# Matrix product of differenced running sums: when the first rows are started, and in which DMA queue their last stores wait

## The chip, the cores and the metric

One core of one Trainium2 chip runs the kernel. The metric is the device time of one execution in microseconds (us). A run here means one execution; a median is over several of them.

## The reference, cut to what matters

```python
# x: (8, 2048, 2048) float32, w: (2048, 2048) float32
cs = np.cumsum(x, axis=1)
diff = cs - shifted(cs)            # shifted by one row, a zero row first
return np.matmul(diff, w)
```

A running sum minus the running sum one row earlier is the row itself. So the kernel computes out = x times w: 16384 rows, 128 row tiles of 128 rows.

## The kernel before

It works in three stages.

1. *First rows.* Row tiles 0 to 3 (512 rows) are multiplied in bf16, while w streams in from memory in 32 blocks: 16 for the left half of the columns, 16 for the right half. TensorE itself transposes this part of x.
2. *First group.* Once all of w is there, it is scaled by its largest magnitude and narrowed to f16. Row tiles 4 to 7 form the first group. From here on the products are by Strassen and Winograd, two levels, so besides matmuls there are sums of quarters of x and w on VectorE (S1 to S4, T1 to T4), evictions of results on ScalarE (`keep`), additions of results on VectorE (`add`), and stores (`put`).
3. *The rest.* Tiles 8 to 127 in groups of four; the group of tiles 8 to 11 is called second.

Before a row tile can be multiplied it passes a chain: load (SyncE queue), magnitude (ScalarE), scale from it (VectorE), narrowing to f16 (ScalarE), and a transposing DMA (SyncE queue), which the program calls a turn. In these traces SyncE's DMAs are in one queue (q1, 345.56 MB in the kernel before), GpSimd's in another (q0, 4.20 MB), and ScalarE's, where it issues any, in a third (q10, 0.52 MB); the text also calls such a queue a ring.

The end of the first rows, where the stores of the right half are put in a queue (cuts marked with `...`):

```python
def put(c, rows, columns):
    nc.gpsimd.dma_start(out2[rows, columns], c)
...
measure_4(PLAIN + 2, x6)                 # magnitude of tile 6, in four pieces
finish_row(1)
...                                      # load of tile 5 into x5
turned_6 = narrow_turn(PLAIN + 2, x6)    # turn of tile 6 (SyncE queue)
x7, _ = after("sp", lambda: bring(PLAIN + 3))   # load of tile 7 (SyncE queue)
finish_row(2)
...
finish_row(3)
with tc.issue_after(turned_6.ins):
    for c, rows, columns in done:        # eight pieces of 256 KB
        put(c, rows, columns)            # GpSimd queue
...
left_over(bank(2))                       # the ninth piece: computed, stored
...                                      # magnitude of tile 5
narrow_turn(PLAIN + 1, x5)               # turn of tile 5 (SyncE queue)
```

The call `issue_after` did not keep these stores behind the turn: in the profile before, GpSimd issues four of them at 68.11 and 71.95 us, and the turn of tile 6 is issued at 74.07.

The first group (`g` is tile 4, `h` is tile 6), with the lines that the argument needs:

```python
product(X, A11g, B11, True)          # tile 4
...
keep(C11g, X, ug)                    # lies where the stored pieces were
product(V, A12g, B21, True)
product(Y, A11h, B11, True)          # tile 6: needs its turn
add(C11g, V, ug)
...
total(S1, A21g, A22g, ADD)           # needs the turn of tile 5
product(Z, A12h, B21, True)
weigh(h + 1, d)                      # magnitude of tile 7: needs its load
...
product(V, S1, T1, True)             # called S1*T1 below
...
weigh(g + 4, a)                      # magnitude of tile 8
product(X, A21g, T3, False)
total(S1, A21h, A22h, ADD)
total(S2, S1, A11h, SUB)
add(C11h, Z, uh)
put(C11h, h, 0)
scale_of(g + 4)                      # scale of tile 8 (VectorE)
ready(g + 4)                         # narrow it
turn(g + 4)                          # turn it
add(C12g, V, ug)
put(C12g, g, 1)
fetch_x(g + 5)                       # load of tile 9
...
weigh(g + 5, c)                      # magnitude of tile 9
scale_of(g + 5)
keep(C22, Z, vh)                     # eviction that a later product waits for
```

## Time and profile before

| quantity | before |
|---|---|
| time, median of 3 (lowest to highest) | 1512.86 us (1511.98 to 1514.31) |
| span of the profiled execution | 1511.4 us |
| TensorE busy | 1493.6 us (99%) |
| VectorE, ScalarE, GpSimd busy | 73%, 57%, 1% |
| hardware queue of SyncE, share of 16 DMA engines | 79.9% |
| first matmul of tile 4 | 72.7 us |
| first matmul of S1*T1 | 95.20 us |
| matmul behind the wait in the second group | 145.12 us |

The last three rows are marks on TensorE's timeline. The kernel is bound by TensorE from end to end, so a change can only be read by how much earlier TensorE passes such a mark. The lines themselves are shown in the prediction. In them `fin` is a loaded row tile of x (tile 5 is loaded into `xP`), `xT` a turned one, `b` a bank of TensorE's results, `c` a result tile, and `o` a stored piece of the first rows (two of them go by `wb`, the name of w's cast blocks). Line numbers move with the change: the eviction is L492 before and L497 after, the addition L497 before and L502 after.

### The profile page before, as it was taken

Reading aid. Unit: us, or ns where it says so; the run is one execution under the profiler, and the core shown is the slowest. Engines: PE = TensorE matmul, PEld = TensorE weight load, DVE = VectorE, ACT = ScalarE, POOL = GpSimd, SP = SyncE. Lnnn points to the kernel's source line nnn. Section 1 sums busy time; section 2 is a strip of 40 time slices with the busy share of each in tenths; the row PEclk is TensorE's granted clock in tenths of the full one; section 3 lists DMA queues with packets and bytes.
Section 4 is the critical chain, followed back from the end, with each engine's and each line's share of the span. In section 5 each row is a group of like instructions: output and inputs, shape, how many; then the busy total and the mean of one; then the engine's idle time right before and its main releaser. Section 6 shows DMA issues by size and latency. Waiting matters only on the chain.

```text
span 1511.4 us, 19128 instructions
## 1 busy us (share of the span) xinstructions
PE 1493.6 (99%) x6906; PEld 674.7 (45%) x6912; DVE 1104.4 (73%) x2052; ACT 866.8 (57%) x1116; POOL 11.9 (1%) x21
## 2 busy tenths in 40 slices
PE   8999999999999999999999999999999999999998
PEld 3434444444444444444444444444444444444443
DVE  7887777676777676776677776767776767777767
ACT  5866555556555656555556555665555565556551
POOL 0200000000000000000000000000000000000000
PEclk9999999999999999999999999999999999999999
DMA  9987878878888888888789788778787888887772
GB/s 362 347 227 232 241 218 249 226 218 235 236 228 237 213 227 237 218 249 235 204 234 242 214 247 223 226 233 240 220 237 211 235 226 240 239 233 218 224 209 111
DMA packets 321903, 351.50 MB, mean 233 GB/s; under 512 B 266896, under 2 KB 266896, under 8 KB 305936
## 3 DMA queue, kind: packets, MB, share of 16 engines
q1 hardware_dynamic: 320240, 345.56, 79.9%
q0 software_dynamic: 1280, 4.20, 0.8%
q8 instruction: 54, 0.88, 0.2%
q10 hardware_dynamic: 288, 0.52, 0.1%
q14 instruction: 41, 0.34, 0.1%
HBM read 150.99 MB, written 134.22 MB: 189 GB/s over the span
## 4 chain that ended last, share of the span: by engine, by line
PE 89%; DVE 1%; issue 0%; DVEq 0%; ACT 0%
PE b L463 53%; PE b L474 36%; DVE c L497 1%; DVE W L506 0%; DVE W L510 0%; DVEq L929 0%; ACT b L548 0%; DVE xT L506 0%; DVE s L112 0%; DVE m L111 0%; DVE u L581 0%; DVE m L556 0%; DVEq L497 0%
## 5 line engine op out<-in xcount | busy, mean ns | idle before, releaser
L497 DVE SCALAR_TENSOR_TENSOR c<-b,u,c 128x512 f32<-128x512 f32 (+1 forms) x883 | 675.2, 800 | 237.4 <-ACT c L492 115.3
L492 ACT ACTIVATE c<-b,u 128x512 f32<-128x512 f32 x496 | 314.8, 679 | 272.7 <-PE b L463 174.8
L463 PE MATMUL b<-W,xT 128*128 128x512 f16 x2048 | 464.1, 380 | 4.3 <-DMA xT<-fin 3.3
L463 PE MATMUL b<-W,W 128*128 128x512 f16 x1764 | 411.7, 379 | 0.0
L105 ACT ACTIVATE c<-fin 128x2048 f16<-128x2048 f32 x92 | 175.6, 1909 | 246.9 <-DMA out_dram<-c 235.9
L463 PEld LDWEIGHTS <-xT 128*128 128x128 f16 x2048 | 200.7, 98 | 248.1 <-DMA xT<-fin 4.5
L463 PEld LDWEIGHTS <-W 128*128 128x128 f16 x2016 | 197.3, 98 | 238.0 <-issue 0.3
L116 ACT ACTIVATE fin<-fin,s 128x2048 f16<-128x2048 f32 x123 | 246.3, 2002 | 88.7 <-issue 49.8
L474 PEld LDWEIGHTS <-W 128*128 128x128 f16 x1560 | 152.2, 98 | 187.0 <-issue 2.0
L474 PE MATMUL b<-W,W 128*128 128x512 f16 x810 | 219.8, 379 | 0.7 <-DVE c L497 0.5
L474 PE MATMUL b<-W,xT 128*128 128x512 f16 x720 | 180.0, 379 | 0.1
L474 PE MATMUL b<-inner,W 128*128 128x512 f16 x660 | 176.2, 379 | 0.0
L474 PEld LDWEIGHTS <-xT 128*128 128x128 f16 x960 | 93.9, 98 | 113.3
L556 DVE TENSOR_REDUCE m<-m 128x1 f32<-128x4 f32 x29 | 4.6, 157 | 103.2 <-ACT b L548 103.2
L463 PE MATMUL b<-W 128*128 128x512 f16 x252 | 74.9, 379 | 0.0
L548 ACT ACTIVATE b<-fin 128x512 f32<-128x512 f32 x116 | 67.9, 585 | 10.1 <-DMA fin<-in_x_dram 9.8
L506 DVE TENSOR_TENSOR W<-W,xT 128x1024 f16<-128x1024 f16 x122 | 68.1, 558 | 3.2
L506 DVE TENSOR_TENSOR W<-xT,W 128x1024 f16<-128x1024 f16 x122 | 67.4, 552 | 0.0
L474 PE MATMUL b<-inner,xT 128*128 128x512 f16 x240 | 61.6, 379 | 0.0
L233 PE MATMUL b<-wb,xP 128*128 128x512 bf16 x234 | 56.0, 388 | 3.7 <-ACT wb L216 2.9
L506 DVE TENSOR_TENSOR W<-xT,xT 128x1024 f16<-128x1024 f16 (+1 forms) x92 | 54.8, 596 | 0.0
L111 DVE TENSOR_SCALAR m<-m 128x1 f32<-128x1 f32 x124 | 18.5, 149 | 37.4 <-ACT c L105 36.2
(55 smaller groups left out, 467.6 us busy)
## 6 DMA issues: line engine op xcount, KB each, us to landing
out_dram<-c SPq DMA_DIRECT2D x247, 512.0 KB, 3.1
fin<-in_x_dram SPq DMA_DIRECT2D x123, 1024.0 KB, 5.5
W<-in_w_dram SPq DMA_DIRECT2D x32, 512.0 KB, 9.3
W<-in_x_dram SPq DMA_DIRECT2D x16, 256.0 KB, 7.5
out_dram<-o POOLq DMA_DIRECT2D x14, 256.0 KB, 5.1
xT<-fin SPq DMA_TRANSPOSE x184, 5.1
xP<-in_x_dram SPq DMA_DIRECT2D x1, 1024.0 KB, 8.0
out_dram<-wb POOLq DMA_DIRECT2D x2, 256.0 KB, 6.9
```

What stands on the lines that cost most here:

```text
L105: return m, nc.scalar.activation(waste.bitcast(f16), xf, ABS, scale=1.0 / ROW, accum_out=m)
L111: nc.vector.tensor_scalar(m, m, TINY, None, MAX)
L116: return xh, nc.scalar.activation(xh, xf, COPY, scale=s)
L233: lambda: nc.tensor.matmul(ps[r][n], xP[:, r, ko, :], wb[h, ko][:, ds(n * NB, NB)], start=(ko == 0), stop=(ko == KO - 1),),
L463: nc.tensor.matmul(ps[n], a[k], b[k][:, n, :], start=(first and k == 0), stop=(k == KH - 1), skip_group_check=True,)
L474: nc.tensor.matmul(ps, a[k], b[k], start=(first and k == 0), stop=(k == 3), skip_group_check=True)
L492: after("act", lambda: nc.scalar.activation(c, p, COPY, scale=scale))
L497: "dve", lambda: nc.vector.scalar_tensor_tensor(c, p, scale, c, MUL, ADD)
L506: after("dve", lambda: nc.vector.tensor_tensor(dst.all, p.all, q.all, op))
L548: lambda: nc.scalar.activation(ps[i % 2], xf[:, at], ABS, scale=1.0 / ROW, accum_out=m4[:, i : i + 1],),
L556: after("dve", lambda: nc.vector.tensor_reduce(m, m4, AX.X, ADD))
```

## The change

The intent: let the first rows begin before all of their x is there; get the stores of the right half out of the way of the turn of tile 6; shorten the way to that turn; and let the magnitude of a tile of the third group go ahead of an eviction. There are four parts. (a) The start: x of rows in pairs around the first block of w.

```diff
-    WARM = 8
+    WARM = 7
...
-        loads = {0: 0, 2: 1, 5: 2, 9: 3}
+        loads = {2: 1, 5: 2, 9: 3}
         for ko in range(KO):
             if ko in loads:
                 load_x(loads[ko])
+            if ko < 2:
+                load_x(0, range(2 * ko, 2 * ko + 2))
             fetch(0, ko)
-        xb = cast_x(0)
-        v = [turn_x(xb, a, 6 + a) for a in range(2)]
-        turned(0, 0, v[0], "act")
-        turned(0, 1, v[1], "dve")
         for ko in range(KO - KQ):
+            if ko == 0:
+                for a in range(2):
+                    xb = cast_x(0, [a])
+                    turned(0, a, turn_x(xb, a, 6 + a), "dve")
+                    if a == 0:
+                        taken(0, ko)
+                    for r in (2 * a, 2 * a + 1):
+                        plain(0, r, ko)
+                continue
```

(b) The stores: from the GpSimd queue to the SyncE queue, behind the turn of tile 6 and ahead of the turn of tile 5. The load of tile 7 goes to the end.

```diff
-            put(c, ds((PLAIN - 1) * P, P), ds(NB, NB))
+            done.append((c, ds((PLAIN - 1) * P, P), ds(NB, NB)))
...
-        turned_6 = narrow_turn(PLAIN + 2, x6)
-        x7, _ = after("sp", lambda: bring(PLAIN + 3))
+        narrow_turn(PLAIN + 2, x6)
...
-        with tc.issue_after(turned_6.ins):
-            for c, rows, columns in done:
-                put(c, rows, columns)
...
         left_over(bank(2))
+        for c, rows, columns in done:
+            after("sp", lambda: put(c, rows, columns, nc.sync))
...
         narrow_turn(PLAIN + 1, x5)
+        x7, _ = after("sp", lambda: bring(PLAIN + 3))
```

(c) Magnitudes of tiles 4 and 6 in two pieces of 1024 instead of four of 512.

```diff
-            for i in range(4):
-                at = ds(i * NB, NB)
+            for i in range(2):
+                at = ds(i * NH, NH)
```

(d) The order of two steps in the second group.

```diff
         product(Y, A11h, B11, True)
+        if second:
+            weigh_in(g + 4, V)
         C11h = new_c(b)
         keep(C11h, Y, uh)
-        weigh_in(g + 4, V)
+        if not second:
+            weigh_in(g + 4, V)
```

More of the change, by code (lines that the diff above doesn't have):

```diff
@@ L172, with load_x @@
             )
-        def load_x(q):
-            for r in range(PLAIN):
+        def load_x(q, rows=range(PLAIN)):
+            for r in rows:
                 nc.sync.dma_start(
@@ L179, in load_x, with cast_x @@
                 )
-        def cast_x(q):
+        def cast_x(q, pairs=range(2)):
             xb = resting(q, 0).bitcast(bf16).rearrange("p (a c) -> p a c", a=2)
-            for a in range(2):
+            for a in pairs:
                 after(
@@ L240, in plain, with put @@
                 )
-        def put(c, rows, columns):
-            nc.gpsimd.dma_start(out2[rows, columns], c)
+        def put(c, rows, columns, queue=nc.gpsimd):
+            return queue.dma_start(out2[rows, columns], c)
         def plain_out(h, r):
@@ L335, in block, with measure_2 @@
                 )
-        waste = first.tile([P, NB], f16, name="waste")
+        waste = first.tile([P, NH], f16, name="waste")
         got = {}
         scales = {}
-        def measure_4(t, xf):
-            m = small.tile([P, 1], f32, name="m")
-            m4 = small.tile([P, 4], f32, name="m4")
-            for i in range(4):
-                at = ds(i * NB, NB)
+        def measure_2(t, xf):
+            m, m2 = (small.tile([P, n], f32, name=i) for n, i in ((1, "m"), (2, "m2")))
+            for i in range(2):
+                at = ds(i * NH, NH)
                 after(
@@ L349, in measure_4 @@
                     lambda: nc.scalar.activation(
-                        waste, xf[:, at], ABS, scale=1.0 / ROW, accum_out=m4[:, i : i + 1]
+                        waste, xf[:, at], ABS, scale=1.0 / ROW, accum_out=m2[:, i : i + 1]
                     ),
                 )
-            after("dve", lambda: nc.vector.tensor_reduce(m, m4, AX.X, ADD))
+            after("dve", lambda: nc.vector.tensor_reduce(m, m2, AX.X, ADD))
             scales[t], _ = after("dve", lambda: invert(m))
@@ L382, in left_over @@
             after("act", lambda: nc.scalar.activation(c, ps, COPY, scale=uw))
-            put(c, ds((PLAIN - 1) * P, P), ds(NB, NB))
+            done.append((c, ds((PLAIN - 1) * P, P), ds(NB, NB)))
         for k in range(4):
             block(B11, 0, 0, k, "dve")
-        measure_4(PLAIN, x4)
+        measure_2(PLAIN, x4)
         for k in range(4, KH):
@@ L393 @@
             block(B21, 1, 0, k, "dve")
-        measure_4(PLAIN + 2, x6)
+        measure_2(PLAIN + 2, x6)
         finish_row(1)
```

## The prediction

> **What bounds the kernel now.** I began with the page. TensorE is nearly full:
>
> ```profile
> PE 1493.6 (99%) x6906; PEld 674.7 (45%) x6912; DVE 1104.4 (73%) x2052; ACT 866.8 (57%) x1116; POOL 11.9 (1%) x21
> ```
>
> The span is 1511.4 us, so everything that could be gained without taking away matmuls is 17.8 us of idle, plus any time in which matmuls run slowly. By stage, TensorE is busy 1305.9 of the last 1312 us; all that this change touches lies before 200 us. The view of TensorE's waits names nearly all of the idle time:
>
> ```profile
> PE b L463 <- DMA xT<-fin: 3.3, 1, 3.3
> PE b L233 <- ACT wb L216: 2.9, 7, 0.8
> PE b L195 <- DVE W L186: 2.6, 1, 2.6
> PE b L258 <- DVE xP L158: 1.2, 1, 1.2
> PE b L463 <- ACT c L492: 0.8, 1, 0.8
> PE b L474 <- DVE c L497: 0.5, 1, 0.5
> ```
>
> One hole of 3.3 us stands out. The timeline around it (start, duration, engine, operation) shows why:
>
> ```profile
> 72.03 2.01 ACT L116 ACTIVATE fin<-fin,s 128x2048 f16<-128x2048 f32 x1
> 74.07 4.84 SPq L127 DMA_TRANSPOSE xT<-fin  x1
> 74.81 3.02 POOL L243 DMA_DIRECT2D out_dram<-o  x4 [1.62 <-ACT o L251]
> 79.00 1.46 SPq L99 DMA_DIRECT2D fin<-in_x_dram  x1
> 82.33 6.83 SPq L127 DMA_TRANSPOSE xT<-xP  x2
> 86.60 8.77 PE L463 MATMUL b<-W,xT 128*128 128x512 f16 x32 [3.35 <-DMA xT<-fin]
> 89.35 1.26 ACT L492 ACTIVATE c<-b,u 128x512 f32<-128x512 f32 x2 [3.93 <-DMA out_dram<-o]
> 90.07 1.41 DVE L497 SCALAR_TENSOR_TENSOR c<-b,u,c 128x512 f32<-128x512 f32 x2 [3.49 <-ACT c L492]
> 92.60 0.68 DVE L506 TENSOR_TENSOR W<-xT,xT 128x1024 f16<-128x1024 f16 x1
> 93.63 1.90 ACT L105 ACTIVATE c<-fin 128x2048 f16<-128x2048 f32 x1
> ```
>
> The turn (transposing DMA) of row tile 6 is issued at 74.07 and lands 12.5 us later, at 86.6, where the turn of tile 4 took 5.5. Between, the GpSimd queue puts in stores of the right half. The same stores then hold ScalarE until 89.35 (the result tile lies where they read), and VectorE until 90.07. From 90 to about 107 us VectorE runs without a real pause, so this late start is carried on.
>
> The hole costs more than itself. Stretches, with busy time and instruction count of each engine, granted clock, DMA share and GB/s:
>
> ```profile
> 83.25:86.60 3.35, 0.00 (x2) 0.01 (x1) 3.33 (x7) 2.17 (x3) 0.00 (x0) 1.00 1.03 412
> 86.60:90.40 3.80, 3.80 (x10) 1.40 (x11) 0.33 (x1) 1.05 (x2) 0.00 (x0) 0.56 1.17 293
> ```
>
> After the hole the clock is 0.56, and ten matmuls take 3.80 us. The 32 matmuls from 86.60 to 95.20 take 8.60 us; at 0.2155 us each (a weight load to the next, in the steady part) they would take 6.90. So 1.70 us more is lost: the hole is worth 3.35 + 1.70 = 5.05 us.
>
> The other place that the change touches:
>
> ```profile
> 138.90 2.00 ACT L116 ACTIVATE fin<-fin,s 128x2048 f16<-128x2048 f32 x1 [0.47 <-ACT c L105]
> 140.81 1.25 ACT L492 ACTIVATE c<-b,u 128x512 f32<-128x512 f32 x2
> 144.40 2.41 ACT L492 ACTIVATE c<-b,u 128x512 f32<-128x512 f32 x4
> 144.53 0.16 DVE L556 TENSOR_REDUCE m<-m 128x1 f32<-128x4 f32 x1 [1.70 <-ACT b L548]
> 145.12 3.61 PE L463 MATMUL b<-W,xT 128*128 128x512 f16 x16 [0.81 <-ACT c L492]
> ```
>
> TensorE waits 0.81 us for an eviction that stands on ScalarE behind four magnitude pieces (141.95 to 144.4).
>
> [...] with stores of another queue beside it a turn took 12.5 us instead of 5.5, at a DMA share over 1.0. It follows that stores put behind the turn in its own ring should no longer stretch it. [...] 3.35 us idle, then 3.8 us at 0.56.
>
> **The change part by part.**
>
> *Start.* x of rows 0 and 1, w block 0, x of rows 2 and 3, w block 1, instead of all x first. Before, the two casts of x start at 5.13 and 8.93 and block 0's cast at 10.39; first matmul 11.48. Now block 0 should take the second place and land near 8.9; cast 1.04, so four matmuls at about 10.0, at the cold 0.43 us each until 11.7. The second x pair lands near 10.4, but its eight turns (1.03 us) stand behind those four, then a VectorE copy of 0.69: about 13.5 before rows 2 and 3 can run. They end near 14.8, where the old order ended block 0 near 14.5. I count nothing. Nor would a small gain last: from 15 to 39.7 us TensorE waits for casts of w in six or seven places, some 2 us together, with DMA at 403 to 409 GB/s, and ScalarE busy 9.71 of the 10 us from 30 to 40. Arrival of w sets this stage. One warm-up matmul less frees 0.6 us before the first turn, in idle time. **0 us, give or take 0.5.**
>
> *Magnitudes by halves.* Four 512-wide pieces of about 0.75 us (61.54 to 64.55 together) become two 1024-wide ones. Width 512 takes 0.62 plus 0.19 for the accumulator, width 2048 takes 1.90 plus 0.19; between them 1.05 plus 0.19, with overlap about 1.17. Twice that is 2.35 against 3.0: 0.65 us each for tiles 4 and 6. For tile 6 this lies on the way to its turn: issue at 73.4 instead of 74.07.
>
> *Stores.* Nine stores of 256 KB leave the GpSimd queue for the SyncE queue, behind turn 6 and before turn 5 (turn of tile 5). Turn 6 then has only the load of tile 5 (issued 69.28) beside it and should take 5.5 to 6 us: landed at 79 to 79.5. TensorE will want it after 16 left-over matmuls and 32 of tile 4, 48 x 0.2155 = 10.3 us after 72.7: at 83.1. Margin over 3 us, so the hole closes and the clock stays: at 95.2 TensorE is up to **5.05 us** ahead.
>
> But can the others follow? ScalarE narrows tile 5 some 0.65 us earlier, so turn 5 is asked for at 81.7. Ahead of it are 9 x 0.262 = 2.36 MB of stores; from 78.5 at 350 to 400 GB/s they last until about 85. Then turn 5 lands at 89.5, near the 90 us at which TensorE wants its sums: a gap of 0 to 0.5 us. The eviction at 89.35 moves to about 85, the VectorE add from 90.07 to about 86. The load of tile 7, issued at 79.0 before, now stands behind turn 5: landing at 91 to 92.5 by adding 2.6 us for 1 MB at 400 GB/s. ScalarE measured tile 7 at 93.63 without a wait; now it starts at 91 to 92.5, and VectorE, which needs that result in the middle of its run, gains only **1.6 to 3 us**.
>
> TensorE has slack against VectorE there (sums ready at 93.3, used at 95.2; 3.8 us for tile 7's sums), so no new hole need appear before 110. But the chain scale of tile 8, its turn, load of tile 9, its magnitude (119.99, waiting for that load), the run of subtractions on VectorE, eviction, magnitude, eviction leads to the wait at 144. It moves with VectorE, by 1.6 to 3 us, plus the 0.49 us by which TensorE was the later at 122.9. TensorE, 5 us ahead by then, will wait there for what is missing: 0.8 + 5.05 - (2 to 3.5) = 2.3 to 3.8 us. So most of what is lost again is lost at this place.
>
> *Order in the second group.* Magnitude pieces go ahead of the eviction of the other bank. The eviction that TensorE waits for has the same work ahead of it in both orders (1.25 + 2.45 us); the VectorE scale behind the pieces comes 1.2 us sooner, but from 150 to 170 TensorE is busy 19.8 of 20 us. **0 to 0.3 us.**
>
> Sum: 0 from the start, 2 to 3.5 kept of 5.05 for the stores, 0 to 0.3 for the order: **about 3.0 us faster, 1509.8 us.** No matmul of the main part is removed, and the instruction order from 200 us on is the same but for buffer names.
>
> **Rivals.** (1) Everything follows TensorE: tile 7 lands in time, and the full 5.05 us plus 0.5 stay: 1507.3. For it: slack of 2 to 4 us nearly everywhere. Against it: the DMA engines are at full share from 70 to 92 us whatever the order; moving stores first puts tile 7 last. (2) The wait only changes place: stores hold turn 5 and tile 7 so long that TensorE stops near 90 for 3 us or more and drops its clock again: 1512.5 to 1514. For it: the two halves of turn 5 held SyncE 6.83 us under load before. Against it: before, 1 MB for tile 7 stood ahead of turn 5, now it doesn't. (3) The start gains 1 to 1.5 us because block 0 is used sooner, and w's casts keep up: 1508.5. Against it: the waits for w after 20 us.
>
> **Range and chances.** I take the mean at 1509.8; rival 1 (chance a quarter) and rival 2 (a sixth) give the edges: 1507.0 to 1512.6, with about 1 us of spread between runs of the kernel before in it. Two per cent is 30 us, more than all idle time of TensorE, so faster by over 2% has 0.5%; slower by as much would need a new wait in the steady part, where order is unchanged: 0.5%.
>
> **What would show it.** Right: no wait for a turned tile near 83; clock 1.0 from 80 to 95; turn 6 lands in 5 to 7 us; TensorE 4 to 5 us ahead at 95; a wait of 2 to 4 us for an eviction near 140. Wrong: first 40 us ending a microsecond or more sooner; a hole at 88 to 92; no longer wait near 140, which would mean that I overrated the load of tile 7; or turn 6 still taking 10 us, which would mean that loads and not stores stretched it.

## The result, and the profile after

The changed kernel took 1509.21 us (median of 4, 1508.53 to 1509.67). The kernel before, run beside it, took 1513.12 us (median of 4, 1511.98 to 1514.31). The ratio is 0.9974, with a 95% interval of 0.9956 to 0.9991. All ratios in this document are the mean time of one kernel's runs over that of the other's of the same rounds, so they are not quite the ratio of the medians quoted. The change is faster, by 0.3%.

The line of busy times from the page of the changed kernel:

```profile
PE 1490.6 (99%) x6911; PEld 673.8 (45%) x6911; DVE 1104.4 (73%) x2053; ACT 864.5 (57%) x1107; POOL 5.2 (0%) x12
```

And TensorE's waits (engine, tile, line, what it waited for: us in total, times, longest):

```profile
PE b L233 <- ACT wb L216: 4.8, 9, 1.0
PE b L468 <- ACT c L497: 2.3, 3, 1.3
...
PE b L233 <- DVE xP L204: 0.8, 1, 0.8
PE b L195 <- DVE W L186: 0.7, 1, 0.7
```

The wait for a turned tile (3.3 us before) is not in the list any more. The wait for x in the start fell from 2.6 to 0.7 us, but the waits for casts of w (`wb`) rose from 2.9 to 4.8 us, and 0.8 us for a turned copy of x is new: 5.5 us together before, 6.3 after. TensorE starts sooner and waits more. Of the 2.3 us for evictions, 0.8 are the old wait and 1.5 are new.

The stretch that had the hole, in the timeline of the changed kernel (start, duration, engine, operation, idle before it):

```profile
72.53 1.84 SPq L127 DMA_TRANSPOSE xT<-fin  x1
...
75.21 13.76 PE L468 MATMUL b<-W,xT 128*128 128x512 f16 x63
76.03 4.72 SPq L243 DMA_DIRECT2D out_dram<-o  x7
80.88 3.25 SPq L127 DMA_TRANSPOSE xT<-xP  x2
84.17 1.35 SPq L99 DMA_DIRECT2D fin<-in_x_dram  x2
84.53 1.26 ACT L497 ACTIVATE c<-b,u 128x512 f32<-128x512 f32 x2 [0.89 <-DMA out_dram<-o]
85.25 1.41 DVE L502 SCALAR_TENSOR_TENSOR c<-b,u,c 128x512 f32<-128x512 f32 x2 [0.46 <-ACT c L497]
...
89.89 1.91 ACT L105 ACTIVATE c<-fin 128x2048 f16<-128x2048 f32 x1 [0.99 <-DMA fin<-in_x_dram]
```

TensorE runs 63 matmuls from 75.21 without a wait, through the place of the hole. The turn of tile 6, issued at 72.53, lands 4.7 us later; it took 12.5 before. Then come the stores, then the turn of tile 5 (80.88), then the load of tile 7 (84.17). The eviction that had waited 3.93 us for stores waits 0.89. The clock stays full in the same stretch (busy times and counts of the engines, clock, DMA share, GB/s):

```profile
75.20:88.80 13.60, 13.60 (x64) 6.17 (x63) 13.08 (x25) 11.97 (x12) 0.00 (x0) 1.00 1.07 304
```

S1*T1 begins at 88.81 instead of 95.20, so TensorE leads by 6.39 us there (of this, about 1.2 us were already there at the first matmul of tile 4, 71.54 against 72.7). At the wait in the second group it leads by only 4.49 us (140.63 against 145.12). Between them 1.9 us are lost again. This is where:

```profile
102.93 2.00 ACT L116 ACTIVATE fin<-fin,s 128x2048 f16<-128x2048 f32 x1 [3.79 <-DVE s L112]
104.96 1.83 SPq L127 DMA_TRANSPOSE xT<-fin  x1
109.23 0.34 SPq L99 DMA_DIRECT2D fin<-in_x_dram  x1
115.76 1.91 ACT L105 ACTIVATE c<-fin 128x2048 f16<-128x2048 f32 x1 [1.94 <-DMA fin<-in_x_dram]
117.67 2.40 ACT L497 ACTIVATE c<-b,u 128x512 f32<-128x512 f32 x4
118.39 0.38 PE L468 MATMUL b<-W,W 128*128 128x512 f16 x1 [1.32 <-ACT c L497]
...
140.63 3.61 PE L468 MATMUL b<-W,xT 128*128 128x512 f16 x16 [0.78 <-ACT c L497]
```

Read it upwards from 118.39. TensorE waits 1.32 us for an eviction (117.67); that stands on ScalarE behind the magnitude of tile 9 (115.76), which waited 1.94 us for its load; the load (109.23) stands in the SyncE queue behind the turn of tile 8 (104.96); and the narrowing before that turn waited 3.79 us for a scale from VectorE (102.93). The wait at 140.63 is 0.78 us, as before (0.81).

### The profile page after: what moved, and what is told of

The parts are those of the page before. It is cut to its first block, busy times and chain, and to the rows that moved or that the text cites. A ratio compares the mean times of both kernels' runs of the same rounds, so it can differ in the third digit from the quotient of the medians.

```text
span 1507.3 us, 19123 instructions
## 1 busy us (share of the span) xinstructions
PE 1490.6 (99%) x6911; PEld 673.8 (45%) x6911; DVE 1104.4 (73%) x2053; ACT 864.5 (57%) x1107; POOL 5.2 (0%) x12
## 4 chain that ended last, share of the span: by engine, by line
PE 88%; DVE 1%; DMA 1%; issue 0%; ACT 0%; DVEq 0%; ACTq 0%; SPq 0%
PE b L468 52%; PE b L479 36%; DVE c L502 1%; DMA fin<-in_x_dram 0%; DMA xT<-fin 0%; DVE W L511 0%; ACT b L553 0%; DVE W L515 0%; ACT c L497 0%; DVEq L937 0%; DVE xT L511 0%; DVE s L112 0%; DVE m L111 0%; DVE u L586 0%; DVE m L561 0%
## 5 line engine op out<-in xcount | busy, mean ns | idle before, releaser
L553 ACT ACTIVATE b<-fin 128x512 f32<-128x512 f32 x116 | 67.8, 585 | 14.5 <-DMA fin<-in_x_dram 14.5
```

Of the source, the lines that this page charges most:

```text
L553: lambda: nc.scalar.activation(ps[i % 2], xf[:, at], ABS, scale=1.0 / ROW, accum_out=m4[:, i : i + 1],),
```

## The experiments

My theory after the first trace: part (b) alone makes the gain, because stores in another ring hold up a turn (12.5 us in the kernel before), and stores behind it in its own ring do not (4.7 us in the changed one). The rivals: the start makes a part of it (in the first pair of traces the first matmul of tile 4 came 1.2 us sooner); the halves or the order make a part; what stretched the turn was the load of tile 7 and not the stores; or GpSimd's queue is peculiar, rather than any second ring. For the 1.9 us given back the theory is the chain just read, from VectorE's place for the scale of tile 8; the rival is the order of magnitude and eviction on ScalarE. The texts below were written before the runs; in them A is the explanation under test and B its rival (in start_only A and B are two rivals and C is the prediction; in order_only A is the prediction).

Twelve kernels ran in three calls, five rounds each, with nine runs of the kernel before in each call (medians 1514.05, 1513.60 and 1514.51 us). Each call ran on another chip, so times are best compared within a call: start_only to order_only; full to x7_late (and both_first); no_start, stores_act, scale_early and best. Eleven gave a correct result, one a wrong one. The marks on TensorE's timeline, from the profiled execution of each (the last column is the time from S1*T1 to the mark in the second group, so what was lost in between shows as an excess over 49.9; both_first and best don't wait at that mark and are left out):

| kernel | time, median us | ratio | first of tile 4 | S1*T1 | second group | difference |
|---|---|---|---|---|---|---|
| before | 1512.86 | | 72.7 | 95.20 | 145.12 | 49.92 |
| changed | 1509.21 | 0.9974 | 71.54 | 88.81 | 140.63 | 51.82 |
| start_only | 1512.82 | 0.9994 | 72.42 | 94.33 | 144.25 | 49.92 |
| stores_only | 1509.71 | 0.9973 | 72.19 | 89.71 | 141.50 | 51.79 |
| halves_only | 1515.06 | 1.0009 | 72.27 | 94.83 | 144.75 | 49.92 |
| order_only | 1513.45 | 1.0000 | 72.27 | 92.35 | 143.78 | 51.43 |
| full | 1509.27 | 0.9970 | 72.62 | 89.89 | 141.79 | 51.90 |
| x7_early | 1512.41 | 0.9992 | 71.93 | 92.17 | 143.63 | 51.46 |
| x7_late | 1514.96 | 1.0006 | 72.44 | 97.99 | 147.91 | 49.92 |
| no_start | 1509.35 | 0.9966 | 72.07 | 89.34 | 141.40 | 52.06 |
| stores_act | 1516.06 | 1.0010 | 71.93 | 95.61 | 147.43 | 51.82 |
| scale_early | 1508.34 | 0.9961 | 72.27 | 89.53 | 139.61 | 50.08 |

### Each part alone

**start_only** is the kernel before with part (a), the diff shown above.

> The kernel before with the first part of the change alone (pairs of x around block 0, one warm-up matmul less). Theory A (from the trace of the full change, where the left-over matmuls began 1.2 us earlier): the first stage ends 1.0 to 1.3 us earlier, and since the turn of tile 6 is asked for earlier by as much, the whole comes out 0.8 to 1.3 us faster (ratio about 0.9993). Theory B: the stage ends earlier, but the landing of the turn of tile 6 stays at 86.6 us, as the stores set it; the hole grows from 3.35 to about 4.5 us and the time is the same within 0.3 us. Theory C, my prediction: the first stage itself gains nothing.

Measured: 1512.82 us (1512.0 to 1514.28), ratio 0.9994 [0.9982, 1.0007]. Worth nothing that five rounds can show. The hole is there: TensorE waits 2.78 us for the turned tile at 85.73.

**no_start** is the converse, the changed kernel with the old start (part (a) reversed).

> The whole change without its first part (x all first, eight warm-up matmuls). If the first part is worth what the first trace of the whole change seemed to show (TensorE 1.2 us earlier at the end of the first stage), this is 0.5 to 1.2 us slower than the whole change (1509.8 to 1510.5). If it is worth nothing, as I predicted, it lies within 0.4 us of it.

Measured: 1509.35 us (1508.04 to 1510.37), ratio 0.9966 [0.9952, 0.9980]; the whole change has 0.9970 and 0.9974. So no part of the gain can be shown to come from the start. The first trace had misled: over all the traces, the first matmul of tile 4 comes on average at 72.3 us with the old start (six traces, 72.07 to 72.7) and at 72.0 with the new one (eight, 71.52 to 72.62). A difference of 0.3 us between means, where single executions differ by 1.1, is not settled by these traces; so most of the 1.2 of the first pair must be put down to chance.

**stores_only** is the kernel before with part (b), the diff shown above.

> The kernel before with the stores alone moved (behind the turn of tile 6 in SyncE's queue, load of tile 7 behind the turn of tile 5). Theory A: the hole of 3.35 us and the slow clock after it are gone, TensorE is 5.0 us ahead at 95 us of the old time, 1.3 to 2 us of it is given back at a wait for an eviction near 120 or 140 us; 3.0 to 3.7 us faster (ratio 0.9976 to 0.9980). Theory B: the hole closes only together with the earlier request (halves); here 0.5 us or more of it stays, and less than 2.5 us is gained.

Measured: 1509.71 us (1509.62 to 1509.90), ratio 0.9973 [0.9961, 0.9986]. That is the gain of the whole change, and more than the 3.0 to 3.7 us that A expected (4.3 by the medians). No hole at 83; S1*T1 at 89.71; and the same loss later: waits of 0.64, 0.94 and 0.20 us between 97 and 120, and 0.78 at 141.50. The five times lie within 0.3 us, where the kernel before ranged over 4.4 us (1511.56 to 1515.94).

**halves_only** is the kernel before with part (c).

> The kernel before with the magnitudes of tiles 4 and 6 in two pieces instead of four. Theory A: the turn of tile 6 is asked for 0.65 us earlier and lands as much earlier, so the hole shrinks by 0.65 us and the time by 0.4 to 0.7 us (ratio 0.9996). Theory B: its landing is set by the stores beside it; the request is earlier, the landing is not, and the time is the same within 0.3 us.

Measured: 1515.06 us (1513.45 to 1516.23), ratio 1.0009 [0.9995, 1.0023]. The turn of tile 6 is issued at 73.26, while the five traces with four pieces have 73.48 to 74.07, so it is asked for 0.2 to 0.8 us sooner. It lands as late as ever, 12.9 us afterwards, and TensorE waits 3.44 us. Here an earlier start gained nothing: B came true.

**order_only** is the kernel before with part (d).

> The kernel before with the magnitude pieces ahead of the eviction in the second group. Theory A (prediction): the wait of 0.8 us near 144 us stays, as the eviction has the same work ahead of it; 0 to 0.3 us. Theory B: the VectorE result that comes 1.2 us sooner is worth up to 1 us, as the chain that ended last runs over VectorE from 144 to 164 us (ratio 0.9993).

Measured: 1513.45 us (1512.2 to 1516.23), ratio 1.0000 [0.9986, 1.0013]. The wait in the second group is 0.78 us (0.81 before), and no gain shows. But its profiled execution is worth reading, because in it the stores happened to be late by themselves. Timeline of this kernel, GpSimd's stores, then an eviction, then TensorE:

```profile
74.23 6.07 POOL L243 DMA_DIRECT2D out_dram<-o  x3 [1.62 <-ACT o L251]
...
88.36 1.26 ACT L492 ACTIVATE c<-b,u 128x512 f32<-128x512 f32 x2 [3.38 <-DMA out_dram<-o]
...
92.35 0.60 PE L463 MATMUL b<-W 128*128 128x512 f16 x2 [2.64 <-DVE W L506]
```

GpSimd takes 6.07 us over the issue of three stores, where in the kernel before it issued four in 3.02. The turn of tile 6 lands after 7.3 us and there is no hole at 83. Then the eviction waits 3.38 us for the late stores, the sum S1 comes late, and TensorE stops for 2.64 us at 92.35 instead. So a kernel with the old stores has two ways to lose time here. That the kernel before takes now one and now the other is inferred from its spread; only one of its executions was profiled. This execution too then lost time later (51.43 in the last column of the table).

### What stretches the turn

**full** is the changed kernel again, unaltered.

> The whole change again, in five rounds, beside the next three on the same chip. The stores alone gave 1509.7 us with a spread of 0.3 us; the whole should then lie at 1508.5 to 1509.5 us, with a spread under 1.5 us, and its trace should again show no wait for a turned tile, and waits of about 1.5 us near 118 us and 0.8 us near 140 us for an eviction. If start, magnitudes and order were worth what their parts were meant to give (1.2 + 0.65 + up to 1), it would lie at 1507.

Measured: 1509.27 us (1508.93 to 1510.75), ratio 0.9970 [0.9957, 0.9982]. Here tile 4 began at 72.62, as before, and S1*T1 came at 89.89: 5.31 us before the old 95.20, with no part of that from the start. Later waits: 0.46, 1.24 and 0.20 us, and 0.78 in the second group. The spread was 1.8 us, where under 1.5 was expected. As its first stage ended when that of the kernel before did, this is the trace to set beside the kernel before. The magnitude of tile 7 in it:

```profile
91.13 1.91 ACT L105 ACTIVATE c<-fin 128x2048 f16<-128x2048 f32 x1 [1.25 <-DMA fin<-in_x_dram]
```

**x7_late** is the kernel before, with only the load of tile 7 moved behind the turn of tile 5. The stores stay on GpSimd.

```diff
-        x7, _ = after("sp", lambda: bring(PLAIN + 3))
...
         narrow_turn(PLAIN + 1, x5)
+        x7, _ = after("sp", lambda: bring(PLAIN + 3))
```

> The kernel before, with the load of tile 7 alone moved behind the turn of tile 5; the stores stay on GpSimd's queue. Theory A (stores beside the turns): the turn of tile 6 or that of tile 5 is still late in most executions, times 1511 to 1516 with a spread of 2 us or more. Theory B (the load): the hole goes, 1510 or less.

Measured: 1514.96 us (1513.43 to 1516.22), ratio 1.0006 [0.9994, 1.0019]. In this trace the hole is larger than in that of the kernel before:

```profile
88.33 9.82 PE L463 MATMUL b<-W,xT 128*128 128x512 f16 x32 [5.36 <-DMA xT<-fin]
```

The turn took 14.5 us, with no load of tile 7 near it. So the load of tile 7 is not what stretches it.

**x7_early** is the changed kernel, with the load of tile 7 right behind the turn of tile 6, ahead of the stores.

```diff
         narrow_turn(PLAIN + 2, x6)
+        x7, _ = after("sp", lambda: bring(PLAIN + 3))
...
         narrow_turn(PLAIN + 1, x5)
-        x7, _ = after("sp", lambda: bring(PLAIN + 3))
```

> The whole change, but the load of tile 7 right behind the turn of tile 6 as before, ahead of the stores. Theory A (the stores beside the turn made the hole): still no hole at 83 us and steady times; the stores and the turn of tile 5 come 2.5 us later, so VectorE's sums come later and TensorE waits 0 to 2 us near 90 us, against about 1 us saved where tile 7's magnitude waited for its load: 1509 to 1511. Theory B (the load of tile 7 behind the turn stretched it): a hole of 2 us or more is back at 83 us.

Measured: 1512.41 us (1511.66 to 1514.13), ratio 0.9992 [0.9978, 1.0006]. The turn of tile 6 takes 4.7 us, as in the changed kernel, although 1 MB stands right behind it in the same ring. But all that comes after is later: the turn of tile 5 is issued at 83.74 (80.88 in the first trace of the changed kernel), and TensorE stops for its sums. The timeline:

```profile
92.17 1.03 PE L468 MATMUL b<-W 128*128 128x512 f16 x2 [2.81 <-DVE W L511]
```

And the stretch that follows (columns as above):

```profile
92.17:94.50 2.33, 2.33 (x6) 0.89 (x7) 2.33 (x4) 2.33 (x4) 0.00 (x0) 0.50 0.64 257
```

That is the second rival of the prediction: 2.81 us of wait, then a stretch at half the clock, with six matmuls in 2.33 us. Theory A had the mechanism, but expected at most 2 us of wait and 1509 to 1511. The place of the load of tile 7 at the very end is worth 3.1 us (1512.41 against 1509.27). So part (b) needs both its moves: without that of the load no gain shows (0.9992 here), without that of the stores none either (1.0006 in x7_late), and with both it is 0.9973 (stores_only).

**stores_act** is the changed kernel, with the stores in ScalarE's own hardware queue instead of SyncE's.

```diff
+        def store():
+            while done:
+                c, rows, columns = done.pop(0)
+                after("act", lambda: put(c, rows, columns, nc.scalar))
...              # called behind the turn of tile 6, finish_row(2), finish_row(3) and left_over
-        for c, rows, columns in done:
-            after("sp", lambda: put(c, rows, columns, nc.sync))
```

> The whole change, but the stores of the right half are issued from ScalarE's own hardware queue, each pair after its evictions and all after the narrowing of tile 6. Theory A: [...] the turn of tile 6 or of tile 5 is late again: a wait of 2 us or more for one of them between 83 and 93 us, 1512 or more, spread over 1.5 us. Theory B: it was GpSimd's software queue in particular: no such wait, and 1509 to 1510.5 us [...].

Measured: 1516.06 us (1515.27 to 1516.46), ratio 1.0010 [0.9997, 1.0022]. The hole is back, with the turn at 10.3 us:

```profile
83.26 12.22 PE L476 MATMUL b<-W,xT 128*128 128x512 f16 x48 [4.26 <-DMA xT<-fin]
```

So it is not peculiar to GpSimd's ring; ScalarE's does it too. The spread of 1.2 us is under the 1.5 that A expected. A limit of this run: the order of instructions moved too. TensorE asked for tile 6 as early as 79 us, and the turn of tile 5 was issued only at 88.18, so only the length of the turn is to be read from it, not the time.

All fourteen traces agree on the length of the turn of tile 6, from issue to landing. With stores in another ring: 12.5 (before), 12.1 (start_only), 12.9 (halves_only), 14.5 (x7_late), 10.3 (stores_act), and 7.3 where GpSimd happened to be late (order_only). With the stores behind it in its own ring: 4.6 to 4.7 us seven times, and 6.0 in stores_only.

The DMA packets in the traces (a turn moves 2048 of 256 bytes) split this length into three. In the kernel before, the first packet starts 3.1 us after the issue, the packets take 7.3 us to the start of the last, and the landing comes 2.1 us after that; in the changed kernel these are 1.2, 2.9 and 0.7 us. So most of the difference (4.4 us) is that the turn's own packets are spread out, 1.4 us that the landing comes later after them, and 1.9 us that they start later. The load of tile 5, ahead of the turn in SyncE's ring, has a part in this: its last packet ends at 77.00 in the kernel before, where the turn's first starts at 77.20, and at 73.22 in the changed one. It is not the whole of it: in halves_only that load had landed at 75.3 (69.01 + 6.3), 2.0 us after the issue of the turn, against 3.2 in the kernel before (69.28 + 8.0, and 74.07), and the turn took 12.9 us all the same.

### Where the lead is given back

**both_first** tests the rival: evictions ahead of magnitudes on ScalarE. In the first group the eviction of C22 goes ahead of the magnitude of tile 9; in the second the pieces of the magnitude go behind the evictions, just ahead of the narrowing that needs them.

```diff
-        weigh(g + 5, c)
-        scale_of(g + 5)
         C22 = new_c(d)
         keep(C22, Z, vh)
+        weigh(g + 5, c)
+        scale_of(g + 5)
...
-        if second:
-            weigh_in(g + 4, V)
...                                  # after keep(C12g, X, ug), keep(C22, Z, vg), add(C22, X, vg):
+        if second:
+            weigh_in(g + 4, Y)
         ready(g + 4)
```

> The whole change, and two evictions put ahead of a magnitude on ScalarE: in the first group the one of the product that is ready before tile 9's magnitude (which waits for its load), in the second group two evictions ahead of the magnitude pieces, whose scratch then is the bank that is free. Theory A: TensorE's lead of 5 to 6 us at 95 us is given back at those two waits only; both vanish (1.5 and 0.8 us) and 1.5 to 2.3 us more is gained: about 1507. Theory B: the load of tile 9 and the run of VectorE behind it are the true limit; the waits come back at another place within 30 us, and less than 0.7 us is gained.

Measured: 1511.13 us (1510.46 to 1512.16), ratio 0.9980 [0.9968, 0.9993], and a **wrong result** (relative error 0.077). The mistake is mine: the pieces need a bank for their unused output, I gave them Y, and Y still holds a partial sum that the next product adds to. Timing can still be read. The wait at 117.77 falls to 0.53 us, but the magnitude of tile 9 starts only at 118.19, 1.3 us later than in full. VectorE has the scale of tile 9 at the head of a run of work without a pause: it begins at 120.22 (118.96 in full) and comes to the first sum of the second group at 132.77 (131.81 in full). TensorE, now 1.8 us ahead of where it is in full, waits for the sums there:

```profile
134.23 1.00 PE L468 MATMUL b<-W,W 128*128 128x512 f16 x2 [1.97 <-DVE W L511]
```

So the order on ScalarE is not what has to be mended: changing it moves the wait and makes it longer, because VectorE is later still. The profile puts the late start of the eviction (117.03) down to TensorE, whose product was done by 110.4. The DMA view shows another cause: the store that frees its result tile, issued at 109.86 behind the load of tile 9, landed 7.1 us later, at 117.0. In full that store landed at 118.1 (110.91 + 7.2), 0.7 us before the eviction, so no order on ScalarE could have gained more than 0.7 there.

**scale_early** tests the theory: in the first group, the scale, narrowing and turn of tile 8 come right behind its magnitude, ahead of two sums and an addition on VectorE.

```diff
         weigh(g + 4, a)
+        scale_of(g + 4)
+        ready(g + 4)
+        turn(g + 4)
         product(X, A21g, T3, False)
         total(S1, A21h, A22h, ADD)
         total(S2, S1, A11h, SUB)
         add(C11h, Z, uh)
         put(C11h, h, 0)
-        scale_of(g + 4)
-        ready(g + 4)
-        turn(g + 4)
```

> The whole change, and in the first group the scale of tile 8, its narrowing and its turn are asked for as soon as its magnitude is there, instead of behind two sums and an addition on VectorE and a store on SyncE (in the whole change ScalarE stood idle 3.8 us before that narrowing). Theory A: the chain tile 8's scale, its turn, load of tile 9, its magnitude, eviction is what takes back TensorE's lead near 118 us; the load of tile 9 lands 3 us sooner, the wait of 1.2 to 1.5 us is gone and 1.0 to 1.7 us is gained over the whole change: about 1508. Theory B: the load of tile 9 is held by the traffic, not by its issue, or the lead is taken back by VectorE within 20 us: same as the whole change within 0.4 us.

Measured: 1508.34 us (1507.11 to 1510.59), ratio 0.9961 [0.9948, 0.9973]. The same chain as above, in this kernel:

```profile
100.53 2.00 ACT L116 ACTIVATE fin<-fin,s 128x2048 f16<-128x2048 f32 x1 [0.95 <-DVE s L112]
...
107.95 0.34 SPq L99 DMA_DIRECT2D fin<-in_x_dram  x1
...
114.74 1.91 ACT L105 ACTIVATE c<-fin 128x2048 f16<-128x2048 f32 x1 [0.56 <-DMA fin<-in_x_dram]
...
117.94 1.24 PE L468 MATMUL b<-W,W 128*128 128x512 f16 x5 [0.20 <-ACT c L497]
...
139.61 3.61 PE L468 MATMUL b<-W,xT 128*128 128x512 f16 x16 [0.78 <-ACT c L497]
```

The narrowing waits 0.95 us for its scale instead of 3.79, the magnitude of tile 9 waits 0.56 us for its load instead of 1.94, and the wait of 1.32 us on TensorE is gone; the 0.20 us that follow it stay. From S1*T1 to the second group it takes 50.08 us, nearly the 49.92 of the kernel before: the lead is kept.

**best** is scale_early, and in the second group the eviction of C12g ahead of the pieces of the magnitude, that of C11h behind them (the free bank V serves for their output).

```diff
-        if second:
-            weigh_in(g + 4, V)
         C11h = new_c(b)
-        keep(C11h, Y, uh)
+        if not second:
+            keep(C11h, Y, uh)
...              # weigh_in and scale_of of the other groups stay here
         keep(C12g, X, ug)
+        if second:
+            weigh_in(g + 4, V)
+            keep(C11h, Y, uh)
+            scale_of(g + 4)
```

> The same, and in the second group the eviction that TensorE waits for goes ahead of the magnitude pieces (the other one behind them), the scratch bank as in the whole change. Theory A: the wait of 0.8 us near 140 us goes too, 0.5 to 0.8 us more than the kernel with the early scale: about 1507. Theory B: the VectorE run from 140 to 164 us starts 1.2 us later again and what is gained is lost in small waits for VectorE there: same as with the early scale.

Measured: 1508.26 us (1507.68 to 1509.09), ratio 0.9959 [0.9946, 0.9971]. The wait of 0.78 us in the second group is gone, but a new one stands a little later:

```profile
146.17 0.59 PE L479 MATMUL b<-W,W 128*128 128x512 f16 x2 [0.63 <-DVE c L502]
```

So this step adds nothing that can be shown. Both kernels beat the kernel before. Against no_start, which is the changed kernel but for the start, they are about 1 us faster by the medians (1509.35), but the intervals of the ratio overlap.

## Why the prediction was right or wrong

1509.8 us was predicted, 1509.21 came. Point by point:

**The stores: right.** The turn of tile 6 was to shrink from 12.5 to between 5.5 and 6 us; it took 4.7. The hole and its slow clock were to vanish, worth 5.05 us at S1*T1; with an equal start it was 5.31 us (full). stores_only has the whole gain by itself. That stores behind the turn in its own ring would no longer stretch it was my estimate: the trace before showed only a turn of 12.5 us with stores of another ring beside it, against 5.5 for that of tile 4. It agrees with the two runs made to test it: a 1 MB load behind the turn in its ring leaves it at 4.7 us (x7_early), and stores in ScalarE's ring stretch it to 10.3 (stores_act). How the rings share the transfers was not shown. The prediction counted the load of tile 5 as standing beside the turn; it stands ahead of it, and in the kernel before the turn's packets start only when it has ended (77.20 and 77.00). The 350 to 400 GB/s for the stores were my estimate too: in the changed kernel the packets of the nine stores run from 76.14 to 83.82 us, 2.36 MB at 307 GB/s.

**The start: right, no gain shown** (no_start, start_only), and for the reason given: what TensorE no longer waits for x, it waits for casts of w. The times worked out were too late: 10.0 us for the first matmuls of block 0 and 13.5 for rows 2 and 3, where the changed kernel has 8.38 and 11.89 (9.37 and 12.87 in full). The 0.43 us for each of the first matmuls is the step from one weight load to the next in the trace before, from 11.87 to 14.85 us; in the steady part the step is 0.216.

**Halves and order: right.** The halves take about 2.35 us for two pieces, as worked out, and by themselves no gain shows. The order shows none either (1.0000); 0 to 0.3 us was forecast, and an interval of 2 us to each side can't tell these apart, but the wait that it was to touch is 0.78 us, where it was 0.81.

**Where the lead is given back: wrong place.** This is the step that failed. The prediction let VectorE gain only 1.6 to 3 us, because tile 7 would be measured from 91 to 92.5 us, and put the whole loss, 2.3 to 3.8 us, on the wait at 144, which would grow from 0.8. That wait stayed at 0.78. The two terms ahead of it were nearly right. With an equal start (full) tile 7 was measured at 91.13, and its scale came at 93.16 instead of 96.34, so VectorE gained 3.2 us, about the same as at the scale of tile 8 (103.73 against 106.88). In the first trace of the changed kernel these gains are 4.4 us, but there the first stage had ended 1.2 us sooner. Against TensorE's lead of 5.3 us in full, VectorE fell short as predicted, but the shortage showed one eviction upstream: in the same chain of scale, turn, load and magnitude that the prediction had named, but at the eviction directly behind the magnitude of tile 9 (1.24 and 0.20 us in full, 1.32 and 0.20 in the first trace), and before that 0.46 us at 97.42 (0.30 at 96.18 in the first trace). I had followed the chain through that eviction on to the next, and not asked whether TensorE would have to wait for it already. scale_early shows that this chain is the cause of the larger wait; the small one ahead of it isn't part of it (best, with the same step, still has 0.34 at 96.20). The sum of the waits between 95 and 145 us is 0.46 + 1.24 + 0.20 + 0.78 = 2.7 us in full and 2.6 in the first trace, within the 2.3 to 3.8 put on the single one: the amount was right and the place wrong.

**The load of tile 7: only one side counted.** Its place at the end was counted as the price of the change, and that price is real: in full its magnitude waits 1.25 us for it. But the other place was not worked out. x7_early shows that it costs 3.1 us more, by the second rival of the prediction.

**The level of the kernel before, and the spread: underrated.** The lead at the second group is 3.3 us in full and 3.6 in stores_only, against 2 to 3.5 kept in the prediction. Yet the medians differ by 4.3 us in each of these. The three runs put the kernel before at 1512.86, while 27 runs have medians of 1513.6 to 1514.5, and the profiled execution of full was the slowest of its five. I had allowed about 1 us of spread between runs before, and no gain from its going away. So that the forecast came within 0.6 us is in part luck: the gain, 3.0 us, was 0.9 to 1.3 us too small, and the level it was taken from 0.3 to 1.7 us too low. Whether the gain beyond that between two traces comes from a smaller spread stays open. The times lay within 0.3 us in stores_only, against 4.4 for the kernel before, but within 1.8 in full, 2.3 in no_start and 3.5 in scale_early, all with the stores behind the turn, and within 1.2 in stores_act, with the stores in another ring. I did not profile several executions of one kernel.

**The first rival**, that everything follows TensorE and 1507.3 us comes out, did not come true by itself; with the scale of tile 8 moved up the medians are 1508.3. The share of the DMA engines that was held against it, full whatever the order, was 1.07, 1.11 and 1.10 before (70 to 80, 80 to 90, 90 to 92 us), and 0.90, 1.09 and 0.95 in the changed kernel.

## What to carry to other kernels

In this kernel the turn that TensorE waits for took 10.3 to 14.5 us with the stores in another ring (7.3 once, where they were issued late), and 4.6 to 6.0 with the same stores behind it in its own. So it is worth a run to put the bulk behind such a transfer in the same ring, in the order in which the results are wanted; and look at what stands ahead of it there. When a hole is closed, follow each engine's lead separately down the timeline, and look at every wait on the way, not at the largest old one: the lead is cut by the first engine whose program order still holds a step behind work that isn't urgent. And a single pair of traces can show a microsecond that isn't there; a run with the part taken out of the whole change settles it.

## What the traces show of the turn and of the clock after a wait

- With 256 KB stores in another ring the turn of one row tile took 10.3 to 14.5 us (7.3 once, where the stores were issued late), and 4.6 to 6.0 us with the same stores behind it in its own ring.
- Most of the long waits of TensorE in these traces were followed by a lower clock: 3.35 us by a clock of 0.56 (before), 2.81 by 0.50 (x7_early), 2.78 by 0.58 (start_only), and 1.97 by 0.51 (both_first), while a wait of 2.64 us once had 1.00 after it (order_only). So in these kernels a wait of 2 us could already be followed by a slow stretch, and the length of the wait alone does not tell whether it will. What decides it was not shown.
